# Four gate tiles back in full products, and weight sums left to accumulating DMAs in one projection, in a one-layer hybrid trunk

## The chip, the cores and the metric

The kernel runs on one core of one Trainium2 chip. The metric is the device time of one execution in microseconds (us), less is better. The five engines are named as the profile names them: PE (TensorE, matrix products), DVE (VectorE), ACT (ScalarE), POOL (GpSimd), SP (SyncE, which only issues DMAs here). "SPq" and "POOLq" are DMAs issued by SP and by POOL.

## The reference

One decoder layer in float32 over 512 tokens of width 1024. Cut to what matters here:

```
h = rmsnorm(x, g_mix)
z = h @ w_in                     # 10 groups of 512 columns, then 3 x 1024 columns of gate logits
merged = sum over 3 branches n of sigmoid(gate_n(h) + b_n) * (branch_n(h) @ w_branch[n])
x = x + merged @ w_o
q = rmsnorm(x, g_xa) @ w_xq ; k, v = rmsnorm(mem, g_mem) @ w_xk, w_xv     # 256 memory tokens
p = softmax(q k^T / 16)          # 4 heads of 256
x = x + (p @ v) @ w_xo
x = x + squared_relu(rmsnorm(x, g_mlp) @ w_up) @ w_down
out = rmsnorm(x, g_fin)
```

The three branches are a short convolution ("cv"), a stick-breaking attention ("sb") and a retention ("rt").

## The kernel before, in words

**Precision.** A float32 operand is split into a high and a low part of the type float32r (`hi` is ACT's copy, `lo` is DVE's subtraction of it), and a product is three matmuls: high times high, high times low, low times high. An output tile of 128 rows by 512 columns over 1024 inputs is thus 8 x 3 = 24 matmuls of 512 columns.

**The weights' way.** All weights come in chunks of 512 KB (128 partitions x 1024 elements) through one stream. SP loads a chunk into one of six buffers `w_raw` (line 215). `parts_of` (lines 112 and 113) makes the parts `w_part` from it: ACT copies the high part, DVE subtracts the low one. There are ten buffers `w_part`, so five pairs of parts. The stream is pumped two steps ahead of the item that uses it (`AHEAD`); a list of items (`plan`) gives the order in which the program is written, and a scheduler then orders the instructions of each engine. On the chip every engine runs its own instructions strictly in that order, each waiting at semaphores.

**The seven-product form.** Where a 2 x 2 block product is wanted, it can be done with seven block products in place of eight, for some additions before and after. Two places use it. Class `Seven` (with `seven`, line 322) computes a pair of gate tiles: four 512-element additions on the weights (lines 128 and 131, in `w_raw`), four steps of parts, 84 matmuls of 256 columns and three additions of 256 columns on results. Class `Wide` (with `items_w`, line 380) is used for the projections w_o, w_xo and w_down: for each 1024 x 1024 block, it makes the products P1, P5, P6, P3, P2, P7, P4 in this order. The weights come as four block kinds B11, B12, B22, B21, each in two halves j = 0 and 1; P1 is made of B11, P5 of the B11 buffer after one addition, P6 after another two (one of them on the B12 buffer, for P7), P4 after one more. With two halves that is eight DVE additions of 128 x 1024 (lines 128 and 131) for each block. The left sides (`Pairs.make`, line 358) are combined the same way from results: `pr`, `pr_b` and `pr_v`.

**The gates.** There are 24 gate tiles, 8 for each branch. The first 12 (`G7` = 12) are plain tiles of 24 matmuls each (`gates`, line 899), the last 12 are six pairs in the seven-product form (`gates7`, line 928). Each item also makes its branch product (`w_br`, 12 matmuls for each tile), takes a sigmoid on ACT (lines 906 and 935) and multiplies and adds into the merged tile `mg` on DVE (lines 890 and 891). When two tiles of the last branch are done, `Pairs.make` builds the left sides for w_o from them. The last four tiles are thus directly ahead of w_o's products.

**The memory attention.** The queries' eight tiles, the second half of the values (`xv1`) and the scores of each head are interleaved (lines 1127 to 1142). `xa_scores` ends in DVE's maximum and ACT's exponential, `xa_transpose` in a cast on ACT and a subtraction on DVE, and `xa_out(h)` multiplies with the values, with four ACT copies and `Pairs.make` behind it. `xa_out` of heads 2 and 3 stand at the end, followed by w_xo's products in `proj_norm` (line 1013).

Of the kernel before, what the change touches and what calls it, by code (L numbers as in the profile page):

```python
# [15 lines left out]
P = 128  # L16
# [5 lines left out]
W = 512  # L22
# [11 lines left out]
RAWS, WBUFS, AHEAD = 6, 10, 2  # L34
G7, UP = 12, 8


@with_exitstack
def trunk_kernel(ctx: ExitStack, tc: tile.TileContext, x, mem, par, rot, dqd, kdec, g_mix, g_xa, g_mem, g_mlp,
# [97 lines left out]


    class Seven:

# [34 lines left out]
    class Wide:  # L175

        def __init__(self, t, c):
            self.loads = [(t, c + i) for i in range(8)]  # L180
# [169 lines left out]
    class Pairs:  # L350
# [27 lines left out]
    TO = dict(P1=(0, 0), P2=(0, 0), P3=(0, 1), P4=(2, 0), P5=(2, 1), P6=(0, 1), P7=(2, 1))  # L378

    def items_w(src, c, pairs, after=lambda p: None):  # L380

# [3 lines left out]
        def part(p, js, n):  # L385
            bank = dict(P2="p2", P5="p3", P3="p3").get(p, "p1")

            def fn(ws):
# [14 lines left out]
                def add(i):  # L403
                    t, h = TO[p]
                    dst = S["x"][t + i][:, h * 512:(h + 1) * 512]
                    dve.tensor_tensor(out=dst, in0=acc[bank, i], in1=dst, op=ALU.add)  # L406
# [7 lines left out]
            item(fn, (Wide, src, c, n, n + len(js)))  # L414

# [17 lines left out]

    def items_m(src, c0, a, done, nt=NT, tok_outer=False):

        chunks = [(Plain, src, c0 + i) for i in range(4)]
        if tok_outer:
            pss = {}
            for t in range(nt):
                def mm(*ws, t=t):  # L440
                    pss[t] = mmps()
                    proj_m(pss[t], ws, a(), t, 0, 8)
                item(mm, *chunks)
                item(lambda t=t: done(t, pss[t]))
        else:
            pss = []
            for i in range(4):
                def fn(w, i=i):
                    for t in range(nt):
                        if i == 0:  # L450
                            pss.append(mmps())
                        proj_m(pss[t], [w], a(), t, 2 * i, 8)
                        if i == 3:
                            done(t, pss[t])
                item(fn, chunks[i])

# [442 lines left out]
    def gates(n, name, ds=range(KT)):  # L899
        for d in ds:  # L900
            def fn(wg, wb, d=d):
# [7 lines left out]
                gated(n, d, ps2, gt)  # L909
            item(fn, (Plain, w_in, 40 + n * KT + d), (Plain, w_br, n * 4 + d // 2))  # L910

# [88 lines left out]
    gates7(1, "sb", range((G7 - KT) // 2, KT // 2))  # L1000
    gates7(2, "rt", range(KT // 2))

# [9 lines left out]

    def proj_norm(src, name, g, beside, after):

# [18 lines left out]

        items_w(src, 0, lambda k: S[name, k // 2].w[k % 2], ends)
        after(lambda t: item(lambda: norm_T(t, S["hT"], t)))
# [92 lines left out]
    for i in range(KT + 4):  # L1128
# [56 lines left out]

    proj_norm(w_xo, "xo", g_mlp, lambda p: None, first_up)

# [100 lines left out]
def _lay_out(i):  # L1288
# [16 lines left out]
        "g_mlp": a["norm_mlp_g"][0], "g_fin": a["final_g"],  # L1305
        "w_in": np.concatenate(secs + [_pack_t(w_in[:, 10 * W:10 * W + G7 * P])], axis=0),
        "w_gate": _pack_s(w_in[:, 10 * W + G7 * P:]),
        "w_br": np.concatenate([_pack_b(a["w_branch"][0, n]) for n in range(3)], axis=0),
# [35 lines left out]
```

## Time and profile before

| | us |
|---|---|
| median of 3 runs | 1028.94 (1028.44 to 1029.39) |
| the profiled execution's own time | 1027.97 |
| its span | 1026.3 |
| PE busy | 995.6 (97%) |
| DVE busy | 734.8 (72%) |
| ACT busy | 533.4 (52%) |
| POOL busy | 64.5 (6%) |

The span is that of the profiled execution, from the first to the last instruction shown; 1.67 us of its time lie outside. In the timelines a row is: start, length, engine, line, operation, output from input, shape, count; in brackets stands the idle time of that engine just before the row and what ended it. A row with a count stands for several instructions in a row. In the windows a row is one stretch of the span, with the busy time and the number of instructions of each engine, the granted PE clock (1.00 is full), the busy share of the DMA engines and GB/s. Matmul rows overlap, since they are pipelined: the spacing of starts counts, not the length.

### The profile page before, as it was taken

The page shows a single profiled execution, that of the slowest core. Times are in us where ns is not written, and L with a number is a line of the kernel's source. Part 1 is how long each engine was busy: PE and PEld are TensorE (multiplying, and loading weights), DVE is VectorE, ACT ScalarE, POOL GpSimd, SP SyncE. Part 2 cuts the span into 40 slices and gives each one's busy share as a digit, 9 for nine tenths or more (in the row PEclk, how much of TensorE's full clock was granted, in tenths as well). Part 3 has the DMA queues.
Part 4 walks back from the last instruction along what each step waited for, and adds up shares of the span by engine and source line. Part 5 has one row for each costly group of instructions (what it writes and reads, how often), then busy time and mean ns, then how long its engine had stood idle before and what let it go on. Part 6 is the DMA issues. An engine that isn't in the chain of part 4 may idle for free.

```text
span 1026.3 us, 13274 instructions
## 1 busy us (share of the span) xinstructions
PE 995.6 (97%) x5030; PEld 843.1 (82%) x5030; DVE 734.8 (72%) x1089; ACT 533.4 (52%) x923; POOL 64.5 (6%) x125
## 2 busy tenths in 40 slices
PE   6999999999999999997999998999999999999996
PEld 5888888878888889996798886779888888888885
DVE  5657787778454787799795459785784786696785
ACT  6456666766422345455474446465553553553543
POOL 1000111223110000001100000000000000000001
PEclk9999999999999999999899999999999999999999
DMA  9242223212132113234544210252034125215212
GB/s 365 107 144 82 82 83 118 81 72 80 62 103 82 63 62 108 78 124 173 172 168 165 83 62 21 80 187 82 21 119 169 42 81 169 79 42 185 82 42 82
DMA packets 30448, 107.84 MB, mean 105 GB/s; under 512 B 3760, under 2 KB 3760, under 8 KB 30384
## 3 DMA queue, kind: packets, MB, share of 16 engines
q1 hardware_dynamic: 27648, 99.63, 27.6%
q0 software_dynamic: 1440, 5.24, 1.5%
q10 hardware_dynamic: 1296, 2.13, 0.6%
q8 instruction: 39, 0.64, 0.3%
q14 instruction: 25, 0.20, 0.1%
HBM read 104.89 MB, written 2.10 MB: 104 GB/s over the span
## 4 chain that ended last, share of the span: by engine, by line
PE 93%; DVE 5%; issue 1%; ACT 1%; DMA 0%; POOL 0%; DVEq 0%; POOLq 0%; SPq 0%; ACTq 0%
PE p L400 21%; PE mm L272 20%; PE mm L273 20%; PE mm L274 20%; PE p L330 5%; DVE w_part L113 1%; PE o L712 1%; PE aT L678 1%; PE at L497 1%; PE z L654 0%; DMA w_raw<-in_w_in_dram 0%; PE z L655 0%; DVE w_raw L128 0%; DVE w_raw L131 0%; PE ro L854 0%
## 5 line engine op out<-in xcount | busy, mean ns | idle before, releaser
L113 DVE TENSOR_TENSOR w_part<-w_raw,w_part 128x1024 fp32r<-128x1024 f32 (+1 forms) x228 | 274.7, 1206 | 156.4 <-ACT w_part L112 149.9
L112 ACT CAST w_part<-w_raw 128x1024 fp32r<-128x1024 f32 (+1 forms) x228 | 236.6, 1040 | 269.8 <-PE mm L273 125.8
L273 PE MATMUL mm<-hT_l,w_part 128*128 128x512 f32 (+1 forms) x704 | 268.4, 382 | 1.7 <-DVE hT_l L262 1.7
L272 PE MATMUL mm<-hT_h,w_part 128*128 128x512 f32 (+1 forms) x704 | 268.0, 383 | 1.1 <-DVE r_qk L775 1.1
L274 PE MATMUL mm<-hT_h,w_part 128*128 128x512 f32 (+1 forms) x704 | 268.2, 382 | 0.0
L400 PE MATMUL p<-w_part,pr 128*128 128x512 f32 x864 | 205.5, 394 | 3.8 <-ACT pr L261 2.7
L400 PEld LDWEIGHTS p<-w_part,pr 128*128 128x128 f32 x864 | 162.4, 190 | 40.1 <-ACT pr L261 3.1
L273 PEld LDWEIGHTS mm<-hT_l,w_part 128*128 128x128 f32 x704 | 132.5, 188 | 25.6 <-DVE hT_l L262 1.9
L272 PEld LDWEIGHTS mm<-hT_h,w_part 128*128 128x128 f32 x704 | 132.0, 188 | 25.8 <-DVE r_qk L775 1.7
L274 PEld LDWEIGHTS mm<-hT_h,w_part 128*128 128x128 f32 x704 | 132.5, 188 | 24.6
L406 DVE TENSOR_TENSOR x<-p,x 128x512 f32<-128x512 f32 x84 | 56.8, 684 | 20.4 <-PE p L400 20.2
L400 PE MATMUL p<-w_part,pr_b 128*128 128x512 f32 x144 | 36.9, 411 | 2.4 <-ACT w_part L112 2.0
L128 DVE TENSOR_TENSOR w_raw<-w_raw 128x1024 f32<-128x1024 f32 (+1 forms) x36 | 37.5, 1041 | 0.5
L131 DVE TENSOR_TENSOR w_raw<-w_raw 128x1024 f32<-128x1024 f32 (+1 forms) x36 | 37.4, 1038 | 0.1
L330 PE MATMUL p<-mix_h,w_part 128*128 128x256 f32 x192 | 37.0, 283 | 0.0
L400 PEld LDWEIGHTS p<-w_part,pr_b 128*128 128x128 f32 x144 | 28.5, 199 | 9.4 <-ACT w_part L112 2.4
L666 DVE TENSOR_TENSOR_SCAN sb_suf<-ones,sb_e 128x128 f32<-128x128 f32 (+3 forms) x32 | 27.4, 857 | 9.5 <-POOL sb_e L645 8.2
L272 PE MATMUL mm<-w_part,xg_h 128*128 128x512 f32 x64 | 26.4, 413 | 7.8 <-ACT xg_h L266 7.8
L330 PEld LDWEIGHTS p<-mix_h,w_part 128*128 128x128 f32 x192 | 31.0, 191 | 0.2
L669 ACT ACTIVATE sb_suf<-sb_suf 128x128 f32<-128x128 f32 (+3 forms) x32 | 15.1, 471 | 29.5 <-DVE sb_suf L668 29.4
L330 PE MATMUL p<-hT_h,w_part 128*128 128x256 f32 x144 | 28.6, 283 | 0.4 <-ACT w_part L112 0.4
L330 PE MATMUL p<-mix_l,w_part 128*128 128x256 f32 x96 | 27.1, 283 | 0.0
(237 smaller groups left out, 1457.4 us busy)
## 6 DMA issues: line engine op xcount, KB each, us to landing
w_raw<-in_w_in_dram SPq DMA_DIRECT2D x52, 512.0 KB, 3.3
w_raw<-in_w_up_dram SPq DMA_DIRECT2D x32, 512.0 KB, 4.0
w_raw<-in_w_down_dram SPq DMA_DIRECT2D x32, 512.0 KB, 3.3
w_raw<-in_w_br_dram SPq DMA_DIRECT2D x12, 512.0 KB, 3.3
w_raw<-in_w_gate_dram SPq DMA_DIRECT2D x12, 512.0 KB, 3.3
w_raw<-in_w_o_dram SPq DMA_DIRECT2D x8, 512.0 KB, 3.7
w_raw<-in_w_xk_dram SPq DMA_DIRECT2D x8, 512.0 KB, 3.3
w_raw<-in_w_xv_dram SPq DMA_DIRECT2D x8, 512.0 KB, 4.2
```

The lines of the kernel that those rows point to most:

```text
L112: act.copy(out=wh, in_=src)
L113: dve.tensor_tensor(out=wl, in0=src, in1=wh.bitcast(F32), op=ALU.subtract)
L128: dve.tensor_tensor(out=out, in0=a, in1=b, op=ALU.subtract)
L131: dve.tensor_tensor(out=out, in0=a, in1=b, op=ALU.add)
L272: te.matmul(ps, lh, rh, start=first, stop=False)
L273: te.matmul(ps, lh, rl, start=False, stop=False)
L274: te.matmul(ps, ll, rh, start=False, stop=last)
L330: te.matmul(ps[:, :256], x[:, k, :], y, start=first and k == 0 and i == 0, stop=k == 3 and i == 2, skip_group_check=True)
L400: te.matmul(acc[bank, i], x, y, start=p in ("P1", "P5", "P2") and j + k + m == 0, stop=j == 1 and k == 1 and m == 2, skip_group_check=True)
L406: dve.tensor_tensor(out=dst, in0=acc[bank, i], in1=dst, op=ALU.add)
L666: dve.tensor_tensor_scan(out=suf[:, :s][:, ::-1], data0=ones[:, :s], data1=e1[:, :s][:, ::-1], initial=0.0, op0=ALU.mult, op1=ALU.add)
L669: act.activation(out=suf[:, :s], in_=suf[:, :s], func=AF.Exp)
```

## The change

There are four edits.

1. `G8` = 20. The tiles 12 to 19 stay in the seven-product form, the last four (branch "rt", d = 4 to 7) are computed as plain tiles again. Their weights move from the tensor `w_gate` to `w_in`, in the same number of bytes.
2. In the seven-product form of the three projections the weights are only added, never subtracted. The signs move to the left sides (`neg`, one `scalar_tensor_tensor` in place of one `tensor_tensor`) and to the additions of the results (`TO` has an operation now).
3. A new class `Summed`, used for w_xo alone. A DVE addition between two weight blocks is replaced by a DMA that POOL issues: it reads the second block from DRAM again and adds it to the buffer `w_raw`, in which the first block lies. There are eight of these, of 512 KB each. Such a DMA may start when the parts of the buffer's former content have been made, and the next parts may be made when it has landed.
4. `xa_out(2)` and `xa_out(3)` move from ahead of w_xo's products to between its first and its second item (P1 with j = 0, and P5 with j = 0).

```diff
-G7, UP = 12, 8
+G7, G8, UP = 12, 20, 8
...
             if p == "P5":
-                minus(b11, b12, b11)
+                plus(b11, b11, b12)
             elif p == "P6":
-                plus(b11, b22, b11)
+                plus(b11, b11, b22)
                 plus(b12, b12, b22)
             elif p == "P4":
-                minus(b11, b21, b11)
+                plus(b11, b11, b21)
             return parts_of(dict(P3=b22, P2=b21, P7=b12).get(p, b11))
+
+    class Summed(Wide):
+        def __init__(self, t, c):
+            super().__init__(t, c)
+            self.need = [n + (n in (1, 3)) for n in self.need]
+
+        def step(self, raw, p, j):
+            b11, b12, b22, b21 = (raw[i] if i < len(raw) else None for i in (2 * j, 2 * j + 1, 4 + j, 6 + j))
+
+            def acc(dst, i):
+                pool.dma_start(out=dst, in_=self.t[self.c + i], accum_op=ALU.add)
+
+            parts = parts_of(dict(P3=b22, P2=b21, P7=b12).get(p, b11))
+            if p == "P1":
+                acc(b11, 2 * j + 1)
+                acc(b12, 4 + j)
+            elif p in ("P5", "P6"):
+                acc(b11, 4 + j if p == "P5" else 6 + j)
+            return parts
...
+            def neg(out, a, b):
+                dve.scalar_tensor_tensor(out=out, in0=a, scalar=-1.0, in1=b, op0=ALU.mult, op1=ALU.subtract)
+
             v = scr("pr_v", (P, 2, 256))
-            minus(v, u[:, 0:1, :].broadcast_to([P, 2, 256]), s)
+            minus(v, s, u[:, 0:1, :].broadcast_to([P, 2, 256]))
             put(("A11", "A22"), s)
-            minus(u[:, 0, :], s[:, 0, :], v[:, 1, :])
+            neg(u[:, 0, :], s[:, 0, :], v[:, 1, :])
             put(("S3", "S1"), v)
...
-            minus(u[:, 1, :], u[:, 1, :], u[:, 0, :])
+            neg(u[:, 1, :], u[:, 1, :], u[:, 0, :])
...
-    gates7(2, "rt", range(KT // 2))
+    gates7(2, "rt", range((G8 - 2 * KT) // 2))
+    gates(2, "rt", range(G8 - 2 * KT, KT))
...
-    item(lambda: xa_out(2))
-    item(lambda: xa_out(3))
+
+    def last_heads(its):
+        plan.append(its.pop(0))
+        item(lambda: xa_out(2))
+        item(lambda: xa_out(3))
+        plan.append(its.pop(0))
...
-    proj_norm(w_xo, "xo", g_mlp, lambda p: None, first_up)
+    proj_norm(w_xo, "xo", g_mlp, lambda p: None, first_up, last_heads, Summed)
```

**What moves.** The first place is DVE at the end of the gates. Before, with the last pair's weights in the buffers 3828 and 3830:

```order
L131 TENSOR_TENSOR w_raw_3828<-w_raw_3830,w_raw_3828 128x512
L262 TENSOR_TENSOR pr_3990<-mg_2676,pr_3990 128x512
L128 TENSOR_TENSOR w_raw_3828<-w_raw_3830,w_raw_3828 128x512
L346 TENSOR_TENSOR sv_u_4026<-p3_4024,sv_u_4026 128x256
L113 TENSOR_TENSOR w_part_4172<-w_raw_3828,w_part_4171 128x1024
L344 TENSOR_TENSOR sv_s_4025<-p1_4022,sv_s_4025 128x256
L113 TENSOR_TENSOR w_part_4176<-w_raw_3830,w_part_4175 128x1024
L113 TENSOR_TENSOR w_part_4184<-w_raw_3836,w_part_4183 128x1024
L890 TENSOR_TENSOR gt_4135<-mm_4138,gt_4135 128x512
L113 TENSOR_TENSOR w_part_4190<-w_raw_4003,w_part_4189 128x1024
L891 TENSOR_TENSOR mg_2809<-mg_2809,gt_4135 128x512
```

After, with the buffers 3836 and 3842, of which 3842 is the first that belongs to w_o:

```order
L910 TENSOR_TENSOR gt_4031<-mm_4033,gt_4031 128x512
L288 TENSOR_TENSOR pr_3985<-pr_v_3979,pr_3985 128x512
L393 SCALAR_TENSOR_TENSOR mg_2676<-mg_2676 128x256
L911 TENSOR_TENSOR mg_2809<-mg_2809,gt_4031 128x512
L113 TENSOR_TENSOR w_part_4121<-w_raw_3842,w_part_4120 128x1024
L910 TENSOR_TENSOR gt_4079<-mm_4081,gt_4079 128x512
L288 TENSOR_TENSOR pr_3991<-mg_2676,pr_3991 128x512
L131 TENSOR_TENSOR w_raw_3842<-w_raw_3842,w_raw_3994 128x1024
L911 TENSOR_TENSOR mg_2809<-mg_2809,gt_4079 128x512
L131 TENSOR_TENSOR w_raw_3994<-w_raw_3994,w_raw_4112 128x1024
```

The four 512-element additions on the last pair's weights and the result additions of lines 342 to 346 are gone; between the subtractions of line 113 there now stand mostly the gates' multiplications (line 910, formerly 890) and the left sides (lines 288 and 393), and the first two additions for w_o (line 131) stand three and five rows behind the low part of w_o's first block (4121).

The second place is POOL from the queries' norm to the norm behind w_xo. Before:

```order
L460 TENSOR_TENSOR rstd_4746<-ms_4744,half_78 128x1
L460 TENSOR_TENSOR rstd_4752<-ms_4750,half_78 128x1
L94 DMA g_bc_6039<-in_g_mlp_dram 128x1024
L460 TENSOR_TENSOR rstd_6096<-ms_6094,half_78 128x1
L460 TENSOR_TENSOR rstd_6102<-ms_6100,half_78 128x1
```

After:

```order
L480 TENSOR_TENSOR rstd_4630<-ms_4628,half_78 128x1
L480 TENSOR_TENSOR rstd_4636<-ms_4634,half_78 128x1
L213 DMA w_raw_5394<-in_w_xo_dram 128x1024
L213 DMA w_raw_5557<-in_w_xo_dram 128x1024
L213 DMA w_raw_5329<-in_w_xo_dram 128x1024 x2
L213 DMA w_raw_5492<-in_w_xo_dram 128x1024 x2
L213 DMA w_raw_5329<-in_w_xo_dram 128x1024
L213 DMA w_raw_5492<-in_w_xo_dram 128x1024
L94 DMA g_bc_5925<-in_g_mlp_dram 128x1024
L480 TENSOR_TENSOR rstd_5982<-ms_5980,half_78 128x1
```

The eight DMAs of line 213 are the accumulations into the B11 buffers (5329 and 5492, three each) and the B12 buffers (5394 and 5557). They stand ahead of the load of the next norm's gain `g_bc` on the same engine.

The third place is ACT around the last casts of the values, `xv_h`, in the memory attention. Before, with 5445 and 5608 as the two B11 buffers of w_xo:

```order
L112 CAST w_part_5890<-w_raw_5608 128x1024
L1092 ACTIVATE x_p_5709,x_sm_5710<-xsc_5693,x_mx_5706 128x256 x2
L261 CAST xpT_5669<-xpp_5716 128x2x256
L261 CAST xv_h_4356<-mm_5679 128x512
L112 CAST w_part_5909<-w_raw_5608 128x1024
L261 CAST xv_h_4357<-mm_5686 128x512
L112 CAST w_part_5929<-w_raw_5445 128x1024
L261 CAST xpT_5769<-xpp_5764 128x2x256
L1092 ACTIVATE x_p_5757,x_sm_5758<-xsc_5741,x_mx_5754 128x256 x2
L1123 COPY xo_s_5820<-mm_5822 128x256
L1124 COPY xo_u_5821<-mm_5822 128x256
L1123 COPY xo_u_5821<-mm_5831 128x256
L1124 COPY xo_s_5820<-mm_5831 128x256
```

After, with 5329 and 5492 as the two B11 buffers:

```order
L112 CAST w_part_5684<-w_raw_5329 128x1024
L112 CAST w_part_5705<-w_raw_5492 128x1024
L1116 ACTIVATE x_p_5593,x_sm_5594<-xsc_5577,x_mx_5590 128x256 x2
L287 CAST xpT_5553<-xpp_5600 128x2x256
L1116 ACTIVATE x_p_5641,x_sm_5642<-xsc_5625,x_mx_5638 128x256 x2
L112 CAST w_part_5796<-w_raw_5492 128x1024
L287 CAST xv_h_4240<-mm_5563 128x512
L112 CAST w_part_5815<-w_raw_5329 128x1024
L287 CAST xv_h_4241<-mm_5570 128x512
L287 CAST xpT_5653<-xpp_5648 128x2x256
L287 CAST xpT_5653<-xpp_5677 128x2x256
L112 CAST w_part_5834<-w_raw_5492 128x1024
L1147 COPY xo_s_5726<-mm_5728 128x256
L1148 COPY xo_u_5727<-mm_5728 128x256
```

The casts of P5, P1 (j = 1), P5 (j = 1) and P6 (line 112) stand at much the same places among the casts of `xpT`, `xv_h` and the copies of the heads; all but P1's now read buffers that an accumulating DMA writes.

More of the change, by code (lines that the diff above doesn't have):

```diff
@@ L179, in __init__ @@
         def __init__(self, t, c):
+            self.t, self.c = t, c
             self.loads = [(t, c + i) for i in range(8)]
@@ L372, in make, with items_w @@
             split(hi, lo, u[:, 1, :])
-            minus(u[:, 1, :], u[:, 1, :], u[:, 0, :])
+            neg(u[:, 1, :], u[:, 1, :], u[:, 0, :])
             put(("S2", "S4"), u)
     LEFT = dict(P1="A11", P2="A12", P3="S4", P4="A22", P5="S1", P6="S2", P7="S3")
-    TO = dict(P1=(0, 0), P2=(0, 0), P3=(0, 1), P4=(2, 0), P5=(2, 1), P6=(0, 1), P7=(2, 1))
-    def items_w(src, c, pairs, after=lambda p: None):
+    TO = dict(P1=(0, 0, plus), P2=(0, 0, plus), P3=(0, 1, minus), P4=(2, 0, plus), P5=(2, 1, minus), P6=(0, 1, minus),
+              P7=(2, 1, minus))
+    def items_w(src, c, pairs, after=lambda p: None, kind=Wide):
         acc = {}
@@ L403, in add @@
                 def add(i):
-                    t, h = TO[p]
+                    t, h, op = TO[p]
                     dst = S["x"][t + i][:, h * 512:(h + 1) * 512]
-                    dve.tensor_tensor(out=dst, in0=acc[bank, i], in1=dst, op=ALU.add)
+                    op(dst, dst, acc[bank, i])
                 rows = p in ("P7", "P4")
@@ L432, in proj_m, with items_m, fn @@
                 mm3(ps, ah[:, sl], al[:, sl], wh[:, j, :], wl[:, j, :], k == 0, k == nk - 1)
[L434 to L455, printed above, removed]
+    def items_m(src, c0, a, done, nt=NT):
+        pss = []
+        for i in range(4):
+            def fn(w, i=i):
+                for t in range(nt):
+                    if i == 0:
+                        pss.append(mmps())
+                    proj_m(pss[t], [w], a(), t, 2 * i, 8)
+                    if i == 3:
+                        done(t, pss[t])
+            item(fn, (Plain, src, c0 + i))
     def rstd_of(ms, n):
@@ L1011, in reload_x, with proj_norm @@
         S["x"] = load_x()
-    def proj_norm(src, name, g, beside, after):
+    def proj_norm(src, name, g, beside, after, first=lambda its: None, kind=Wide):
         def ends(p):
@@ L1032, in ends @@
             beside(p)
-        items_w(src, 0, lambda k: S[name, k // 2].w[k % 2], ends)
+        its = capture(lambda: items_w(src, 0, lambda k: S[name, k // 2].w[k % 2], ends, kind))
+        first(its)
+        plan.extend(its)
         after(lambda t: item(lambda: norm_T(t, S["hT"], t)))
```

9 lines of the change are left out of this document (5 added, 4 removed).

## The prediction

> **What bounds the kernel now.** I read the page's shares first, then the chain of waits, then PE's timeline and the windows around the two places that the change touches.
>
> ```profile
> PE 995.6 (97%) x5030; PEld 843.1 (82%) x5030; DVE 734.8 (72%) x1089; ACT 533.4 (52%) x923; POOL 64.5 (6%) x125
> ...
> PE 93%; DVE 5%; issue 1%; ACT 1%; DMA 0%; POOL 0%; DVEq 0%; POOLq 0%; SPq 0%; ACTq 0%
> ```
>
> PE sets the time nearly everywhere, and only 5% of the chain goes over DVE. So time is to be had in two ways: fewer PE cycles, or a stretch in which PE waits for DVE. The cost of PE work is read off long runs in the chain of waits (start, length, what):
>
> ```profile
> 432.10 8.63 PE p L330 x72
> ...
> 745.32 32.64 PE p L400 x144
> ```
>
> A 512-column matmul costs 32.64/144 = 0.2267 us, a 256-column one 8.63/72 = 0.1199 us. Where PE waits, its timeline shows. The end of the gates and the first products of w_o:
>
> ```profile
> 475.61 2.79 PE L400 MATMUL p<-w_part,pr 128*128 128x512 f32 x11 [0.34 <-ACT gt L935]
> 481.09 2.90 PE L400 MATMUL p<-w_part,pr 128*128 128x512 f32 x10 [2.69 <-ACT pr L261]
> 484.19 0.73 PE L400 MATMUL p<-w_part,pr 128*128 128x512 f32 x2 [0.21 <-DVE pr L262]
> 486.94 1.22 PE L400 MATMUL p<-w_part,pr_b 128*128 128x512 f32 x2 [2.01 <-ACT w_part L112]
> 488.54 4.62 PE L400 MATMUL p<-w_part,pr_b 128*128 128x512 f32 x10 [0.38 <-DVE w_part L113]
> 492.97 4.28 PE L400 MATMUL p<-w_part,pr 128*128 128x512 f32 x18
> ```
>
> From 475.61 to the start of P6 at 492.97, 17.36 us, PE issues 11+10+2+2+10 = 35 matmuls, 7.9 us at 0.2267. So 9.4 us are lost. What DVE and the clock do meanwhile stands in the windows:
>
> ```profile
> 476.00:480.00 4.00, 2.40 (x11) 1.64 (x9) 4.00 (x6) 1.78 (x3) 0.00 (x0) 1.00 0.00 0
> 480.00:484.00 4.00, 2.84 (x10) 1.72 (x10) 4.00 (x7) 2.71 (x4) 0.00 (x0) 1.00 0.09 18
> 484.00:488.00 4.00, 1.79 (x4) 0.80 (x4) 4.00 (x6) 1.67 (x2) 0.00 (x0) 0.77 0.62 222
> 488.00:492.00 4.00, 3.62 (x9) 2.82 (x9) 4.00 (x6) 0.00 (x0) 0.00 (x0) 0.50 0.45 153
> 492.00:496.00 4.00, 4.00 (x17) 3.21 (x17) 1.31 (x3) 1.05 (x1) 0.00 (x0) 0.87 0.01 4
> ```
>
> DVE is busy for 4.00 of 4 us while PE is not: it is the bound here. And the granted clock falls to 0.50. (0.23+0.50+0.13) x 4 us x 2 = 6.9 us ran at half clock; the ten matmuls at 488.54 took 4.43 us to the next row's start in place of 2.27. About 2.4 us of the 9.4 are the clock's, 7 are waits.
>
> The second place is w_xo's start, with the last values and heads:
>
> ```profile
> 634.70 0.73 PE L274 MATMUL mm<-xpT,xv_l 128*128 128x512 f32 x2 [0.73 <-DVE xv_l L262]
> 639.18 0.66 PE L1104 MATMUL xpp<-ident,x_p 128*128 128x128 f32 x2 [3.75 <-DVE x_p L1096]
> 639.50 5.88 PE L400 MATMUL p<-w_part,pr 128*128 128x512 f32 x17
> ...
> 655.43 2.94 PE L400 MATMUL p<-w_part,pr 128*128 128x512 f32 x11 [0.42 <-DVE pr L262]
> ```
>
> ```profile
> 635.00:640.00 5.00, 1.25 (x5) 0.82 (x4) 5.00 (x10) 2.85 (x9) 0.00 (x0) 0.64 0.00 0
> 640.00:645.00 5.00, 5.00 (x17) 3.89 (x16) 1.69 (x4) 1.59 (x2) 0.00 (x0) 0.68 0.00 0
> ```
>
> Again DVE is full (5.00 of 5) while PE has 1.25, and the clock is halved behind it: (0.36+0.32) x 5 x 2 = 6.8 us. The three waits make 4.9 us, the clock some 1.9 (17 matmuls in about 5.7 us, not 3.85), the tails of the matmuls ahead of the gaps the rest: about 7.3 us lost before P6 of w_xo starts at about 655.9.
>
> **The change, part by part.**
>
> *Four plain gate tiles.* On PE a pair costs 48 x 0.2267 = 10.9 us in full products, 84 x 0.1199 = 10.1 in seven. Two pairs: **+1.6 us**, with nothing to hide it. What DVE is spared stands in the groups by shape from 425 to 500 us:
>
> ```profile
> L113 DVE TENSOR_TENSOR w_part<-w_raw,w_part 128x1024 fp32r<-128x1024 f32 x19 | 23.1, 1218 | 5.0 <-ACT w_part L112 5.0
> ...
> L128 DVE TENSOR_TENSOR w_raw<-w_raw 128x512 f32<-128x512 f32 x4 | 2.7, 685 | 0.0
> ...
> L113 DVE TENSOR_TENSOR w_part<-w_raw,w_part 128x512 fp32r<-128x512 f32 x2 | 1.4, 692 | 0.8 <-ACT w_part L112 0.7
> L346 DVE TENSOR_TENSOR sv_u<-p,sv_u 128x256 f32<-128x256 f32 x3 | 1.3, 419 | 0.6 <-PE p L330 0.6
> ```
>
> For a seven-product pair: four additions of 0.685, one low part of 0.69 and three of 1.22, three result additions of 0.42, together 8.3 us. A plain pair has two low parts, 2.4. Two pairs free 11.8 us of DVE by lengths, some 11 by the closer spacing of starts. The 7 us of waits depend on DVE, so more is freed than lost; but a second limit is behind it. P2's first weight block, made ahead of P6 in both orders, is loaded last:
>
> ```profile
> 482.62 3.34 SPq L215 DMA_DIRECT2D w_raw<-in_w_o_dram  x2
> ```
> ```profile
> 485.84 1.04 ACT L112 CAST w_part<-w_raw 128x1024 fp32r<-128x1024 f32 x1 [0.72 <-DMA w_raw<-in_w_o_dram]
> ```
>
> The load goes out when a buffer is free (482.62), the cast follows at 485.84, the subtraction after that. I laid the new order out by hand with these lengths. By spacings alone PE has P5 (j = 1) behind it at 481.2 (the extra 1.6 is in that). The load is then already there, but the cast needs the two part buffers that P5 holds: high part at 483.1, low part at 485.2 (one other DVE operation of 1.13 between). PE waits 1.9 and 1.6 us, and P6 starts at about 487.5: **-5.5 us** against 492.97, the 1.6 included. If the half clock comes again in these 6.9 us, with PE busy through it, it takes 3.4 back: **-2.1**. Before, it followed on waits of 2.69 and 2.01 us within 8 us, and in w_xo on 0.73 and 3.75. Waits of 1.9 and 1.6 us that close together look like the first of these, so I take -2.1 and keep -5.5 for the range.
>
> The sign changes cost nothing: one 256-column DVE operation is swapped for another, as many as before.
>
> *Eight accumulating DMAs.* They spare DVE eight additions of 1.21 us in w_xo; six of these stand ahead of 640 us, in the stretch where PE waits:
>
> ```profile
> L131 DVE TENSOR_TENSOR w_raw<-w_raw 128x1024 f32<-128x1024 f32 x4 | 4.9, 1214 | 0.0
> ...
> L128 DVE TENSOR_TENSOR w_raw<-w_raw 128x1024 f32<-128x1024 f32 x2 | 2.4, 1214 | 0.0
> ```
>
> That is 7.3 us off a DVE that is full, about the whole loss. The price is a wait: parts, accumulate, parts, in series. No row shows an accumulating DMA. Its time d from issue to landing is bounded by the plain ones of the same size:
>
> ```profile
> w_raw<-in_w_xo_dram SPq DMA_DIRECT2D x8, 512.0 KB, 3.2
> ...
> x<-in_x_dram POOLq DMA_DIRECT2D x4, 512.0 KB, 5.4
> ...
> g_bc<-in_g_xa_dram POOLq DMA_DIRECT2D x1, 512.0 KB, 7.1
> g_bc<-in_g_mlp_dram POOLq DMA_DIRECT2D x1, 512.0 KB, 4.0
> ```
> ```profile
> 468.00:472.00 4.00, 4.00 (x30) 3.78 (x30) 4.00 (x7) 2.21 (x5) 1.60 (x3) 1.00 0.98 366
> ```
>
> Below: 3.2 us, the plain load by SP. Above: 7.1 plus a whole second transfer behind it, 3.2: 10.3. I take 4.0 (a lone load by POOL) plus 512 KB more at the 366 GB/s of the busiest window, 1.4, since the target is read as well: **d = 5.4**, which is also the row of four loads in a run.
>
> The Trainium skill ("DMA: Bandwidth & Descriptors", section "Anatomy of one DMA — SWDGE (gpsimd) path") fits a DMA of this path with 2.0 us and its bytes over 436 GB/s. As an estimate that gives 3.2 us for 512 KB and 4.4 with the target counted, and my sum below would be some 1.7 us better; the row of 4.0 for a plain load lies above the 3.2.
>
> The chain starts at P1's first parts:
>
> ```profile
> 614.03 1.05 ACT L112 CAST w_part<-w_raw 128x1024 fp32r<-128x1024 f32 x1 [3.97 <-PE mm L273]
> ```
> ```profile
> 615.12 1.23 DVE L113 TENSOR_TENSOR w_part<-w_raw,w_part 128x1024 fp32r<-128x1024 f32 x1 [3.60 <-ACT w_part L112]
> ```
>
> The addition for P5 goes out at 616.4 and lands at 621.8; cast and subtraction to 624.0; P1 (j = 1) to 625.8; its addition lands at 631.2, P5 (j = 1) has parts at 633.4; the next addition lands at 638.8 and P6 (j = 1) is cast until 639.8. These casts stand in ACT's order ahead of `xv_h`, `xpT` and the copies of head 2, which wait with them, and DVE and POOL are in order too. In this stretch PE has the two heads' 24 matmuls and the 24 of P1 and P5 (j = 0) to do. By spacings it then waits 1.6 us at P1 (j = 1) and 1 to 1.5 at P5 (j = 1), and P6 starts at about 650.6: **-5.3** against 655.9. By the same layout d = 4.5 gives 648.9, 6 gives 652, 8 gives 656 to 658, 10 gives 664. *The moved heads* are in these figures; alone they only give PE P1's 12 matmuls (2.7 us) ahead of the wait. P4's two additions, late and long landed, free 2.3 us of DVE where PE does not wait: nothing. The gain's load stands behind the eight DMAs on POOL, is issued at about 640 to 645 by this layout and takes 4.0 us; it is first read in the norm behind P3, which comes after P6's 48 matmuls (10.9 us): nothing.
>
> Sum against the profiled execution: 1027.97 - 2.1 - 5.3 = 1020.6. That execution lies 0.97 below the median 1028.94, so about **1021.5** as a median.
>
> **The rivals.**
>
> *The clock stays up behind the gates.* Then the first term is -5.5 and the second stays: 1028.94 - 5.5 - 5.3 = 1018.1. For it: the longest wait falls from 2.69 to 1.9 us. Against it: in the windows above the clock fell though PE had been busy 2.84 and 1.79 of 4 us. The Trainium skill ("TensorE: Matmul & The Clock Gate", section "Part 1: The HAM clock gate (the "warmup" mystery)") ties the half clock to windows of 3.4 us of PE's activity; by its warning against idle gaps longer than that, no wait in the new layout would bring it. The trace of before does not agree, with half clock behind gaps of 2.01 and 2.69 us.
>
> *The accumulations take 7 to 8 us.* Then the series of three eats what DVE gains, and w_xo's P6 is where it was: 1028.94 - 2.1 - 0 to 1 = 1026.4.
>
> *They take longer and the change loses.* The same series at d = 10 puts P6 at 664, +8: 1028.94 - 2.1 + 8 = 1034.8. The place is ACT's cast of P5 (j = 1), behind which the value casts queue; from d = 8.6 on the whole is slower (7.5 if the half clock recurs). For it: 7.1 us for a plain load in one row, and that the two DMAs for P7 go out on the same queue just before. Against it: the DMA engines are idle at 635 to 645 (0 GB/s).
>
> *The gates' end is not relieved.* The part buffers and the last load set P6 of w_o wherever DVE is, the extra 1.6 us is paid, and of w_xo's gain some 1 to 2 us remain: about 1028.
>
> **How the numbers follow.** The forecast has 0.40, the clock that stays up 0.22, the accumulations of 7 to 8 us 0.15, the slower case 0.14, no relief 0.09. About 0.2%, 2 us, is what a measurement of this kernel can tell from no change. Faster: 0.40 + 0.22 + half of 0.15 + 0.02 of the last = 0.72. Slower: 0.14 + 0.01. Same: 0.13. The forecast's own range is 1019.5 to 1024 (d from 4.5 to 6.5, half clock partly). The range runs from 1016.5 (both gains in full, d at 4.5) to 1029, which leaves out the slower case.
>
> **What the changed profile would show.** The accumulate's row from issue to landing, 4.5 to 6.5 us, decides the second term. In w_o, P6 starts near 487.5 at full clock or 491 at half; the wait for P2's cast remains, at about 2 us, and DVE has idle time between 476 and 492. In w_xo, DVE is no longer full at 630 to 640, ACT's casts of P5 and P6 are ended by a DMA, and P6 starts about 5 us earlier relative to the queries' projection. A half clock at 481 to 495 tells the forecast from its first rival. The forecast is wrong if ACT's casts wait more than 4 us for a DMA while PE waits for `xv_h`, or if P6 of w_o starts no earlier than before.

## The result

| | before | after |
|---|---|---|
| median, us | 1028.69 (4 runs, 1027.80 to 1029.39) | 1018.91 (4 runs, 1018.13 to 1020.44) |
| profiled execution, us | 1027.97 | 1020.44 |
| its span, us | 1026.3 | 1018.7 |

The ratio is 0.9913, with a 95% interval of 0.9901 to 0.9925: faster by about 9 us (the two medians are 9.8 us apart). The forecast was 1021.5 with a range of 1016.5 to 1029; the first rival, with a clock that stays up, was at 1018.1. The measured time lies between the two, 0.6 us below the forecast's own narrower range of 1019.5 to 1024.

PE's timeline after the change, at the end of the gates and the first products of w_o (P1 and P5 are the 48, then half of P2, then P6):

```profile
469.97 11.04 PE L430 MATMUL p<-w_part,pr 128*128 128x512 f32 x48
482.38 0.73 PE L430 MATMUL p<-w_part,pr_b 128*128 128x512 f32 x2 [1.36 <-ACT w_part L112]
484.48 3.87 PE L430 MATMUL p<-w_part,pr_b 128*128 128x512 f32 x10 [1.37 <-DVE w_part L113]
488.14 4.16 PE L430 MATMUL p<-w_part,pr 128*128 128x512 f32 x16
```

P1 and P5 run without a wait now, and two waits for P2's parts are left. P6 starts at 488.14 in place of 492.97, **4.8 us** earlier. Of this, 0.4 us lies ahead of the place: the last branch's first product with `rt_out` starts at 410.48 in place of 410.90. The windows there:

```profile
476.00:480.00 4.00, 4.00 (x20) 3.30 (x19) 2.93 (x6) 1.72 (x3) 0.00 (x0) 1.00 0.25 76
480.00:484.00 4.00, 1.75 (x7) 0.81 (x5) 3.68 (x4) 1.85 (x3) 0.00 (x0) 1.00 0.49 160
484.00:488.00 4.00, 3.52 (x10) 2.79 (x11) 3.98 (x6) 0.04 (x1) 0.00 (x0) 0.68 0.46 160
488.00:492.00 4.00, 4.00 (x17) 3.24 (x17) 1.80 (x2) 1.00 (x1) 0.00 (x0) 0.89 0.17 52
```

PE is busy for all of 476 to 480, where it had 2.40 us before. The half clock (a granted clock of 0.50) is back, but shorter: (0.32 + 0.11) x 4 x 2 = 3.4 us of it, where 6.9 had been. The ten matmuls at 484.48 take 3.66 us instead of 2.27, so it costs 1.4 us there.

The DMA view and POOL's timeline show the new transfers (the first row: median us from issue to landing at its end; the others: the first, third and eighth of the eight):

```profile
w_raw<-in_w_xo_dram POOLq DMA_DIRECT2D x8, 512.0 KB, 5.2
```
```profile
575.47 0.93 POOL L213 DMA_DIRECT2D w_raw<-in_w_xo_dram  x1 [53.55 <-DVE x_sm L1118]
...
612.66 0.87 POOL L213 DMA_DIRECT2D w_raw<-in_w_xo_dram  x1 [22.10 <-DVE w_part L113]
...
638.61 0.88 POOL L213 DMA_DIRECT2D w_raw<-in_w_xo_dram  x1 [5.08 <-DVE w_part L113]
```

ACT's casts of weights at the start of w_xo (P1; P5; P1 and P5 with j = 1 third and fourth; P6 with j = 1), and PE's waits up to P6, with which the row of 48 begins:

```profile
610.05 1.05 ACT L112 CAST w_part<-w_raw 128x1024 fp32r<-128x1024 f32 x1 [3.98 <-PE mm L299]
617.88 1.05 ACT L112 CAST w_part<-w_raw 128x1024 fp32r<-128x1024 f32 x1 [1.21 <-PE xsc L300]
619.73 1.05 ACT L112 CAST w_part<-w_raw 128x1024 fp32r<-128x1024 f32 x1 [0.80 <-PE mm L299]
628.32 1.05 ACT L112 CAST w_part<-w_raw 128x1024 fp32r<-128x1024 f32 x1 [3.04 <-DMA w_raw<-in_w_xo_dram]
...
636.00 1.05 ACT L112 CAST w_part<-w_raw 128x1024 fp32r<-128x1024 f32 x1 [3.74 <-DMA w_raw<-in_w_xo_dram]
```
```profile
642.79 2.83 PE L430 MATMUL p<-w_part,pr 128*128 128x512 f32 x10 [0.85 <-ACT pr L287]
646.04 0.73 PE L430 MATMUL p<-w_part,pr 128*128 128x512 f32 x2 [0.42 <-DVE pr L288]
647.24 11.22 PE L430 MATMUL p<-w_part,pr 128*128 128x512 f32 x48 [0.47 <-DVE x L131]
```

From P1's cast to P6 it is 647.24 - 610.05 = 37.2 us; before it was 655.9 - 614.03 = 41.9. That is **4.7 us**. Two casts do wait for an accumulating DMA, for 3.0 and 3.7 us, but PE waits for neither: the largest wait left is 0.85, where 3.75 was. DVE is no longer full there, and the half clock that followed the old wait (6.8 us) does not come, so part of the 4.7 us, some 1.9 by the prediction's reading of before, is the clock's:

```profile
630.00:635.00 5.00, 5.00 (x24) 3.94 (x23) 4.16 (x6) 2.26 (x4) 1.73 (x2) 1.00 0.55 95
635.00:640.00 5.00, 5.00 (x24) 4.12 (x23) 2.91 (x5) 3.82 (x9) 1.39 (x2) 1.00 0.63 116
```

The two gains make 9.5 us and the span is 7.6 shorter. Of the rest, 0.85 went between P6 of w_o and w_xo's first cast (121.9 us in place of 121.1; the half clock's end in P6 and a wait of 0.38), and 1.1 behind P6 of w_xo, in the norm. There PE waits equally long in both kernels, and only the second execution was given a half clock behind it:

```profile
688.55 0.38 PE L273 MATMUL mm<-hT_l,w_part 128*128 128x256 f32 x1 [1.74 <-DVE hT_l L262]
```
```profile
679.81 0.44 PE L299 MATMUL mm<-hT_l,w_part 128*128 128x256 f32 x1 [1.75 <-DVE hT_l L288]
```
```profile
680.00:690.00 10.00, 10.00 (x73) 10.00 (x73) 3.86 (x10) 1.61 (x5) 0.54 (x1) 0.83 0.21 72
```

The first row is the kernel before, the second and the window are after (0.17 x 10 x 2 = 3.4 us at half clock). The profiled execution is the slowest of the four: their granted clocks were 0.995, 0.997, 0.998 and 0.998, their times 1020.44, 1019.49, 1018.34 and 1018.13.

### The profile page after: what moved, and what is told of

Same layout as the page of the kernel before. It is cut to its first block, busy times and chain, and to the rows that moved or that the text cites. A ratio compares the mean times of both kernels' runs of the same rounds, so it can differ in the third digit from the quotient of the medians.

```text
span 1018.7 us, 13121 instructions
## 1 busy us (share of the span) xinstructions
PE 994.7 (98%) x4958; PEld 840.6 (83%) x4958; DVE 717.3 (70%) x1063; ACT 527.3 (52%) x909; POOL 73.7 (7%) x133
## 5 line engine op out<-in xcount | busy, mean ns | idle before, releaser
L299 PE MATMUL mm<-hT_l,w_part 128*128 128x512 f32 (+1 forms) x736 | 281.8, 383 | 1.7 <-DVE hT_l L288 1.7
L300 PE MATMUL mm<-hT_h,w_part 128*128 128x512 f32 (+1 forms) x736 | 281.6, 383 | 0.0
L298 PE MATMUL mm<-hT_h,w_part 128*128 128x512 f32 (+1 forms) x736 | 280.5, 384 | 1.1 <-DVE r_qk L795 1.1
L299 PEld LDWEIGHTS mm<-hT_l,w_part 128*128 128x128 f32 x736 | 139.4, 189 | 26.9 <-DVE hT_l L288 1.9
L300 PEld LDWEIGHTS mm<-hT_h,w_part 128*128 128x128 f32 x736 | 139.4, 189 | 25.6
L298 PEld LDWEIGHTS mm<-hT_h,w_part 128*128 128x128 f32 x736 | 138.3, 189 | 27.0 <-DVE r_qk L795 1.8
L131 DVE TENSOR_TENSOR w_raw<-w_raw 128x1024 f32<-128x1024 f32 (+1 forms) x48 | 54.3, 1131 | 0.7 <-DMA w_raw<-in_w_down_dram 0.3
L128 DVE TENSOR_TENSOR x<-x,p 128x512 f32<-128x512 f32 x48 | 32.6, 683 | 9.5 <-PE p L430 9.5
L298 PE MATMUL mm<-w_part,xg_h 128*128 128x512 f32 x64 | 26.4, 413 | 7.6 <-ACT xg_h L292 7.6
L131 DVE TENSOR_TENSOR x<-x,p 128x512 f32<-128x512 f32 x36 | 24.1, 682 | 11.5 <-PE p L430 11.4
L299 PE MATMUL mm<-w_part,xg_h 128*128 128x512 f32 x64 | 25.8, 404 | 0.0
L356 PE MATMUL p<-mix_h,w_part 128*128 128x256 f32 x128 | 25.0, 283 | 0.0
L300 PE MATMUL mm<-w_part,xg_l 128*128 128x512 f32 x64 | 24.3, 389 | 0.0
L486 ACT ACTIVATE xn<-x 128x512 f32<-128x512 f32 x24 | 15.1, 629 | 15.8 <-DVE x L131 8.0
```

The lines of the kernel that those rows point to most:

```text
L128: dve.tensor_tensor(out=out, in0=a, in1=b, op=ALU.subtract)
L131: dve.tensor_tensor(out=out, in0=a, in1=b, op=ALU.add)
L298: te.matmul(ps, lh, rh, start=first, stop=False)
L299: te.matmul(ps, lh, rl, start=False, stop=False)
L300: te.matmul(ps, ll, rh, start=False, stop=last)
L356: te.matmul(ps[:, :256], x[:, k, :], y, start=first and k == 0 and i == 0, stop=k == 3 and i == 2, skip_group_check=True)
```

## The experiments

The kernel before had medians of 1028.42, 1027.78, 1027.51 and 1028.13 us in the four groups of runs (e1 to e4; e5 to e7; e8 to e10; e11). The changed kernel was not timed again in them under its own name (but see e3).

### The gates alone

```diff
-    proj_norm(w_xo, "xo", g_mlp, lambda p: None, first_up, last_heads, Summed)
+    item(lambda: xa_out(2))
+    item(lambda: xa_out(3))
+    proj_norm(w_xo, "xo", g_mlp, lambda p: None, first_up)
```

> The four plain gate tiles and the sums-only signs alone; the attention's output projection adds on DVE and the last heads stand ahead of it, as before. Theory (two separate gains, each where DVE was full while PE waited): P6 of w_o starts about 4.8 us earlier than before, w_xo is as before: about 1024 us (1022 to 1025.5) against 1028.7 before and 1018.9 with all parts. Rival (the end of the gates gives nothing, all comes from w_xo): 1028 us or more, as PE has 1.6 us more to do.

Measured: 1023.92 us, ratio 0.9955 (0.9943 to 0.9967), that is -4.5 us by the medians, as the theory had it. P6 of w_o started at 488.10. The run shows that the gates' edit gives this time. That it gives it through DVE's time, and not through something else in which the two forms differ, rests on the windows and on e6; it was not tried by itself.

### w_xo alone

```diff
-G7, G8, UP = 12, 20, 8
+G7, G8, UP = 12, 24, 8
```

> All twelve late gate tiles stay in the seven-product form; the accumulating DMAs and the moved heads alone. Theory: P6 of w_xo starts 4.5 to 5.5 us earlier relative to P1's first cast, the end of the gates is as before (waits of 2 to 3 us, half clock): about 1024 us (1022.5 to 1025). Rival (accumulations as slow as 7 us or more, the gain comes from the gates): 1028 us. Second rival (the two gains are one, a half clock that is shed): 1020 us.

Measured: 1024.61 us, ratio 0.9955 (0.9942 to 0.9968), -4.6 by the ratio and -3.8 by the medians. From P1's first cast to P6 of w_xo it is 652.68 - 615.25 = 37.4 us, 4.4 less than before. The two ratios multiply to 0.9910, the whole change has 0.9913: two separate gains of about the same size, and no third.

### The heads back, the sums by DMA

```diff
-    proj_norm(w_xo, "xo", g_mlp, lambda p: None, first_up, last_heads, Summed)
+    item(lambda: xa_out(2))
+    item(lambda: xa_out(3))
+    proj_norm(w_xo, "xo", g_mlp, lambda p: None, first_up, kind=Summed)
```

> All of the change but the moved heads: the last two heads stand ahead of w_xo's first product again, the sums are by DMA. Theory (the heads are cover for the wait on the accumulations of P5): PE does the same work earlier and then waits at P5 or P1 (j = 1) for parts; P6 of w_xo starts 1 to 3 us later, 1020 to 1022 us. Rival (the heads' place carries the gain in w_xo): 1023.5 us or more. Third (place is of no matter, as the chain of casts sets P6): 1018.9 us within 0.7.

Measured: 1018.70 us (6 runs, 1017.51 to 1023.32), ratio 0.9912 (0.9896 to 0.9928). The third: it makes no difference. The reason is plainer than the one I gave: with buffer numbers and line numbers left out, the instructions of all five engines stand in the same order as in the changed kernel. The scheduler had put the last heads there anyway. So this is the changed kernel once more, and its profile shows what the clock adds. In its timeline P2's waits are nearly the same as in the first fence of the result:

```profile
482.59 0.73 PE L430 MATMUL p<-w_part,pr_b 128*128 128x512 f32 x2 [1.41 <-ACT w_part L112]
484.65 2.56 PE L430 MATMUL p<-w_part,pr_b 128*128 128x512 f32 x10 [1.33 <-DVE w_part L113]
487.04 11.04 PE L430 MATMUL p<-w_part,pr 128*128 128x512 f32 x48
```

No stretch between 440 and 700 us is below full clock in this execution (1017.51 us, clock 0.998); the ten matmuls take 2.39 us and P6 starts 1.1 us earlier still.

### The heads moved, the sums on DVE

```diff
-    proj_norm(w_xo, "xo", g_mlp, lambda p: None, first_up, last_heads, Summed)
+    proj_norm(w_xo, "xo", g_mlp, lambda p: None, first_up, last_heads, Wide)
```

> All of the change but the DMAs: w_xo's eight additions are on DVE again, the heads stay between P1 and P5. Theory (DVE's seven us of additions are the gain): DVE is full again at the start of w_xo and PE waits there 3 us or more; 1022.5 to 1024.5 us. Rival (the heads' place carries the gain): 1019 to 1020.5 us.

Measured: 1024.20 us, ratio 0.9960 (0.9948 to 0.9972), within 0.3 us of the gates alone, whose order of instructions it shares (numbers left out). Without the DMAs the old wait is back in PE's timeline:

```profile
635.28 0.41 PE L1128 MATMUL xpp<-ident,x_p 128*128 128x128 f32 x2 [3.75 <-DVE x_p L1120]
```

So all of w_xo's gain comes from the DMAs. (The heads' place may matter in a program in which the scheduler would not choose it; that was not tried.)

### The signs alone

```diff
-G7, G8, UP = 12, 20, 8
+G7, G8, UP = 12, 24, 8
...
-    proj_norm(w_xo, "xo", g_mlp, lambda p: None, first_up, last_heads, Summed)
+    item(lambda: xa_out(2))
+    item(lambda: xa_out(3))
+    proj_norm(w_xo, "xo", g_mlp, lambda p: None, first_up)
```

> The sums-only signs alone: weights are added, never subtracted, the left sides and the result additions carry the signs; gates, additions by DVE and the heads' place as before. Theory (one DVE operation for another of the same shape): no change, 1027 to 1029.5 us. Rival (the swapped operation is slower): more than 1030 us.

Measured: 1027.76 us, ratio 1.0000 (0.9991 to 1.0009). No change, as laid out.

### The price of the series doubled

```diff
             def acc(dst, i):
-                pool.dma_start(out=dst, in_=self.t[self.c + i], accum_op=ALU.add)
+                for _ in range(2):
+                    pool.dma_start(out=dst, in_=self.t[self.c + i], accum_op=ALU.add)
```

> Each accumulating DMA of w_xo is issued twice in a row into the same buffer (the block is added twice, so the output is another one). This doubles the price in the series parts, accumulate, parts. Theory (three accumulations in series, some 2 us of slack in all): the cast of P5 (j = 1) comes some 8 to 10 us later and the value casts behind it in ACT's order with it; P6 of w_xo 8 to 13 us later, 1027 to 1032 us, no longer faster than before (1028.4). Rival (the series is covered by other work): 1019 to 1021 us.

Measured: 1029.70 us (10 runs), ratio 1.0030 (1.0016 to 1.0043): the change becomes a loss, 10.8 us above the changed kernel's median. ACT's cast of P5 (j = 1), the first row, comes 29.6 us behind P1's cast (609.04) in place of 18.3, and P6 45.9 behind it in place of 37.2. PE waits for a left side and for P1's addition to x, which ACT and DVE reach late behind such casts:

```profile
638.66 1.99 ACT L112 CAST w_part<-w_raw 128x1024 fp32r<-128x1024 f32 x2 [5.20 <-DMA w_raw<-in_w_xo_dram]
```
```profile
642.45 7.39 PE L431 MATMUL p<-w_part,pr 128*128 128x512 f32 x24 [2.31 <-ACT pr L288]
654.93 13.81 PE L431 MATMUL p<-w_part,pr 128*128 128x512 f32 x48 [5.09 <-DVE x L131]
```

### A little more for each link

```diff
                 pool.dma_start(out=dst, in_=self.t[self.c + i], accum_op=ALU.add)
+                pool.dma_start(out=dst[:, :128], in_=self.t[self.c + i][:, :128], accum_op=ALU.add)
```

> Behind each accumulating DMA a second one of 64 KB into the first 128 columns of the same buffer (added twice there, so the output is another one): a small addition to the price, about 2.5 to 3.5 us for each link of the series. Theory: 1022 to 1026 us, between the change and no gain in w_xo (1024.2), about what the layout gave for accumulations of 8 us. Rival (covered): 1019 to 1020 us.

Measured: 1027.86 us (10 runs), ratio 0.9998 (0.9989 to 1.0006), worse than I expected: 64 KB more for each link cost 9 us, almost as much as 512 KB. POOL's timeline tells why (the rows from the third pair on; line 213 is the whole accumulation, 214 the small one):

```profile
612.11 0.86 POOL L213 DMA_DIRECT2D w_raw<-in_w_xo_dram  x1 [16.68 <-DVE w_part L113]
617.53 0.86 POOL L214 DMA_DIRECT2D w_raw<-in_w_xo_dram  x1 [4.56 <-DMA w_raw<-in_w_xo_dram]
622.90 0.87 POOL L213 DMA_DIRECT2D w_raw<-in_w_xo_dram  x1 [4.50 <-DVE x_sm L1119]
624.76 0.87 POOL L213 DMA_DIRECT2D w_raw<-in_w_xo_dram  x1 [0.99 <-DVE w_part L113]
628.31 0.87 POOL L214 DMA_DIRECT2D w_raw<-in_w_xo_dram  x1 [2.68 <-DMA w_raw<-in_w_xo_dram]
631.17 0.87 POOL L214 DMA_DIRECT2D w_raw<-in_w_xo_dram  x1 [1.99 <-DMA w_raw<-in_w_xo_dram]
```

The first link takes 5.4 us to the small one's issue and 2.7 (its median) to landing: 8.1, as meant. But the next two accumulations are in flight together, and POOL is in order: the small one of the second buffer (631.17) goes out only behind the wait for the first buffer's (628.31). That is read from the order on POOL; it was not tried with the two on separate queues. The second of these links is 631.17 + 2.7 - 624.76 = 9.1 us or more. Waits of PE for 3.14 and 2.54 us follow. So little of the price is covered by other work, and each wait on POOL's queue belongs to it. Part of the 9 us may be the clock's: from 630 to 700 us this execution has 10.3 us of half clock (the run before it 10.2), the changed kernel 3.4, and each microsecond of it costs a busy PE half of one.

### One plain pair instead of two

```diff
-G7, G8, UP = 12, 20, 8
+G7, G8, UP = 12, 22, 8
```

> Only the last pair of gate tiles is plain, ten of the twelve late tiles stay in the seven-product form: 0.8 us less of PE, 5.5 us instead of 11 of DVE freed. Theory (DVE's excess at the end of the gates is about 7 us, so one pair frees most of it): P6 of w_o within 1.5 us of the change's, 1018 to 1020.5 us. Rival (both pairs are needed): 1021.5 us or more, halfway to 1024.6.

Measured: 1022.04 us, ratio 0.9941 (0.9928 to 0.9954). The theory missed on the time and the rival is right: both pairs are needed. Windows of this kernel, and PE's row of the ten matmuls ahead of P6:

```profile
476.00:480.00 4.00, 2.80 (x13) 1.99 (x11) 4.00 (x8) 2.54 (x3) 0.00 (x0) 1.00 0.40 162
480.00:484.00 4.00, 2.65 (x6) 1.65 (x7) 4.00 (x8) 2.49 (x4) 0.00 (x0) 0.65 0.36 131
484.00:488.00 4.00, 3.72 (x9) 2.15 (x7) 4.00 (x6) 1.67 (x2) 0.00 (x0) 0.50 0.05 9
```
```profile
488.67 2.60 PE L430 MATMUL p<-w_part,pr_b 128*128 128x512 f32 x10 [0.40 <-DVE w_part L113]
```

DVE is still full to 488 us, and PE still waits for it: these ten matmuls start at 488.67, where the change starts them at 484.48. The half clock is back for (0.35 + 0.50) x 4 x 2 = 6.8 us, and P6 starts at 491.10. That is 3.0 us later than in the change, of which 1.3 were there already at the first product with `rt_out` (411.78 against 410.48). So 5.5 us off DVE did not empty it, though PE's waits had come to no more than 7. That buffers covered the rest of DVE's excess is the likely reason; it was not shown.

### The accumulating DMAs in w_o too

```diff
-    proj_norm(w_o, "mp", g_xa, mem_beside, kv_proj)
+    proj_norm(w_o, "mp", g_xa, mem_beside, kv_proj, kind=Summed)
```

> The accumulating DMAs in w_o as well as in w_xo. DVE is spared another 9 us, but there the blocks come late: P1's first part is cast shortly before PE wants it, and three accumulations of some 5 us and three pairs of parts then stand in series ahead of P6's second half. Theory: PE waits 5 us or more for these, 1022 to 1030 us. Rival (DVE's additions are still what P6 of w_o waits for): 1016 to 1018 us.

Measured: 1025.57 us, ratio 0.9971 (0.9960 to 0.9982), 6 to 7 us worse than the change. The wait of PE is there, but behind something I had not named:

```profile
490.11 4.93 PE L430 MATMUL p<-w_part,pr 128*128 128x512 f32 x12 [7.05 <-DVE x L131]
```
```profile
481.91 0.87 POOL L213 DMA_DIRECT2D w_raw<-in_w_o_dram  x1 [4.47 <-DVE w_part L113]
482.45 2.46 POOL L100 DMA_DIRECT2D x<-in_x_dram  x4
```

PE waits for P1's addition into x, and x itself is reloaded by POOL, behind the eight accumulations: at 482, where the change does it between 441 and 464. The next run takes that away.

### w_o too, with x reloaded earlier

```diff
     gates(2, "rt", range(G8 - 2 * KT, KT))
+    plan.insert(len(plan) - 2, ((), lambda: S.update(x=load_x())))
...
-    item(reload_x)
...
-    proj_norm(w_o, "mp", g_xa, mem_beside, kv_proj)
+    proj_norm(w_o, "mp", g_xa, mem_beside, kv_proj, kind=Summed)
```

> As the run before with accumulating DMAs in w_o too, but the reload of x is written two items earlier, so that on POOL it stands between the accumulations instead of behind all of them. There P1's addition to x had kept PE waiting for 7.05 us. Theory (that wait was POOL's order, not the sums): it is gone, P6 of w_o starts near 483 to 485 us instead of 488.1 in the change, as the products before it were done at 483.1; 1014 to 1017.5 us. Rival (the series of accumulations sets P6 of w_o whatever comes behind it): 1019 us or more.

Measured: 1025.49 us, ratio 0.9977 (0.9965 to 0.9989): the same time with other waits. The first waits are gone and P6 begins at 481.75, as hoped; then P2's parts are late.

```profile
481.75 2.97 PE L430 MATMUL p<-w_part,pr 128*128 128x512 f32 x12 [0.62 <-DVE x L131]
...
497.13 0.73 PE L430 MATMUL p<-w_part,pr_b 128*128 128x512 f32 x2 [2.63 <-ACT w_part L112]
```
```profile
484.14 2.94 ACT L112 CAST w_part<-w_raw 128x1024 fp32r<-128x1024 f32 x3 [4.83 <-DMA w_raw<-in_w_o_dram]
...
496.04 1.04 ACT L112 CAST w_part<-w_raw 128x1024 fp32r<-128x1024 f32 x1 [4.08 <-DMA w_raw<-in_w_o_dram]
```

ACT's casts wait 4 to 5 us for DMAs, and one of these is P2's block. The first of the two waits is for an accumulation, issued at 478.63 and landed at 484.06; P3's casts stand behind it in the row of three. The second is for P2's plain load, which SP issues at 488.21, when DVE has made P3's low part and a buffer is free:

```profile
488.21 2.06 SPq L241 DMA_DIRECT2D w_raw<-in_w_o_dram  x2
```
```profile
490.00:495.00 5.00, 4.50 (x20) 3.38 (x18) 3.39 (x7) 1.95 (x8) 1.67 (x3) 1.00 1.03 279
```

That load takes 7.8 us to land, 3.2 in the change: the DMA engines are full, with POOL's loads of `g_bc` and `m_sb` and two accumulations in flight (10.6 and 12.8 us from issue to landing). So POOL's order was one cause. The next is the series, which delays P2's load through ACT's order, and the full DMA engines, which stretch it.

### w_o too, all twelve late tiles in seven products

```diff
-G7, G8, UP = 12, 20, 8
+G7, G8, UP = 12, 24, 8
...
+    plan.insert(len(plan) - 4, ((), lambda: S.update(x=load_x())))
...
-    item(reload_x)
...
-    proj_norm(w_o, "mp", g_xa, mem_beside, kv_proj)
+    proj_norm(w_o, "mp", g_xa, mem_beside, kv_proj, kind=Summed)
```

> Accumulating DMAs in both projections, x reloaded ahead of them, and all twelve late gate tiles in the seven-product form: DVE is spared w_o's additions instead of the gates', PE has 1.6 us less to do than in the change. Theory (at the end of the gates P1's parts of w_o come late from a full DVE, and the series of three accumulations starts from there): P6 of w_o at about 490 us, 1020 to 1024 us. Rival (any 9 us off DVE are worth the same there): 1013 to 1016 us.

Measured: 1030.79 us, ratio 1.0028 (1.0017 to 1.0038): slower than before, by more than I expected. PE waits 2.69 us at 472.27 and 2.08 at 481.51, both for casts, and P6 starts at about 492. Time off DVE is not worth the same in each form: in w_o it is bought with a series of accumulations, which took up to 8.8 us each there. How the loss comes about in this run was not followed further.

### P2 last in w_o

```diff
-                        acc[bank, i] = (mmps if p == "P2" else atps)(bank)
+                        acc[bank, i] = (mmps if p == "P2" and src is not w_o else atps)(bank)
```

> The change with one more edit: in w_o P2's two result banks are taken from the four banks that P1 and P3 use, not from those of the plain products. P2 can then only start when P3's banks are free, and PE takes P6 straight behind P5, with P2's 24 matmuls behind P7 and P4; the sum is the same. Theory (what is left of the loss at the end of the gates is the wait for P2's parts, 1.36 + 1.37 us, and the half clock behind it): P6 starts at 481 to 483 us in place of 488.1, 1015 to 1017.5 us. Rival (P2's parts then hold two of five pairs of buffers through P7 and P4, the wait moves there): 1018.5 us or more.

Measured: 1024.97 us, ratio 0.9970 (0.9960 to 0.9980), 6 us worse than the change. The rival is right that it loses, though not where it said:

```profile
486.17 16.69 PE L430 MATMUL p<-w_part,pr 128*128 128x512 f32 x62 [4.06 <-DVE x L131]
...
534.32 1.09 PE L517 MATMUL at<-ident,xn 128*128 128x128 f32 x8 [2.06 <-DVE hT_l L288]
```

P6 cannot follow P5 at once, since its bank holds P1's result until DVE has added it to x: PE waits 4.06 us there, more than for P2's parts (1.36 + 1.37). And the norm, which needs P2's sum, then ends late (2.06). Between 480 and 495 us it has 6.8 us of half clock, the change 3.4. The order that the scheduler had chosen was the better one.

## Why the prediction was right, and where it was not

**What bounds the kernel** was read rightly: two stretches in which DVE was full and PE waited. Each part relieves one of them, by 4.6 us in a run of its own (by the ratios; 4.5 and 3.8 by the medians), and together they give the whole.

**The gates' end.** P6 at 487.5 was laid out at full clock, 488.14 came with some half clock and 487.04 without (in e3, the same program). The two waits for P2's parts were put at 1.9 and 1.6 us and are 1.36 and 1.37. The term that was mis-sized is the half clock: I took back 3.4 us for a full return of 6.9 us of it; it took 1.4 in the profiled execution and nothing in others. The term is -4.5 in place of -2.1. The second term was 0.7 us too large, so the two errors cancel in part; that the forecast came as near as 2.6 us owes something to this. The +1.6 us of PE is in it and was not measured by itself.

**The accumulations.** d was taken as 5.4 us from the lone POOL load and a second transfer; 5.2 was measured. Counted from P1's first cast, the layout had the three accumulations of the series land at 7.8, 17.2 and 24.8 us and P6 start at 36.6; the trace has 7.8, 18.2, 25.9 and 37.2. P6 was put at -5.3; it is -4.7 in the trace and -4.6 by e2. The cast of P5 (j = 1) waits for its DMA, as laid out, and the value casts behind it do not hold PE up. What failed here is where PE waits: the 1.6 us at P1 (j = 1) and 1 to 1.5 at P5 (j = 1) do not come, and instead there are 0.85, 0.42 and 0.47 ahead of P6, for left sides and for x. The two DMAs for P7, counted for a rival as going out just before, are issued at 575.47 and 589.69, far ahead of the series.

**The moved heads** were a step that failed. I gave them a place in the layout and said that alone they give PE cover. They change nothing here: the order of the instructions is the same without the edit. The orders shown ahead of the prediction are those of the whole change, and can't tell which edit moved what.

**The rivals.** The clock that stays up (1018.1) is close to the truth for some executions. Accumulations of 7 us or more were refuted (5.0 to 5.9 for the eight), and the slower case lives at the price I gave it or below: it was to decide from d = 8.6 on, and links of about 8 to 9 us already cost all of w_xo's gain and the gates' beside it (1027.86). I had left POOL's order out of that price. "The gates' end is not relieved" was refuted by e1.

**The clock rule.** The Trainium skill ("TensorE: Matmul & The Clock Gate", section "Part 1: The HAM clock gate (the "warmup" mystery)") says that the activity window runs freely and does not start with the kernel, so that the point of a transition varies. The traces fit that: one order of instructions with waits of 1.36 + 1.37 us was given 3.4 us of half clock in one execution, and with 1.41 + 1.33 none in another. Its warning against gaps above 3.4 us is too mild for this case, as half clock follows on gaps half as long (1.36 and 1.37 us, and a single one of 1.75).

## What to carry to other kernels

Where a second engine is full while the first waits, look for the work of that engine that can be had in another form right there, and pay with what is cheap there: here 1.6 us of a PE that waited, and DMA engines that had nothing to do. A DMA in a series parts, transfer, parts costs its latency each time. It paid where the chain starts early and other work lies beside it (w_xo), and in none of the three forms tried where the blocks come late (w_o); the order of everything else on the issuing queue belongs to its price. How much has to be taken off the full engine can't be read from the waits alone: half the relief at the gates (e6, ratio 0.9941) left DVE full and brought about a third of what the whole of it did (0.9955 without, 0.9913 with). That share is rough, since each ratio is known to 0.0013; by the medians it is 2.6 of 5.7 us.

## What the hardware showed that was not expected

An accumulating DMA of 512 KB took 5.2 us from issue to landing, against 3.3 for the plain loads of the same tensor by SP. POOL needed 0.87 to 0.97 us to issue one, and 0.54 to 0.58 for most plain loads. Behind plain loads on POOL's queue, with the DMA engines full, two accumulations took 10.8 and 12.8 us to land (e8). The DMA engines were busier for the same traffic (after the change, in w_xo; at the end of the row the busy share and GB/s):

```profile
620.00:625.00 5.00, 5.00 (x31) 4.42 (x30) 3.46 (x9) 2.91 (x9) 1.84 (x2) 1.00 0.61 105
```

That is a share of 0.61 at 105 GB/s, where plain loads of the kernel before had 0.33 at 116 GB/s (440 to 450 us). And the half clock came behind waits as short as 1.36 and 1.37 us in a row, or did not, in the same program. Where it came, it came in pieces of about 3.4 us: between 470 and 720 us the executions have none (e3), 3.4 (e8), 6.8 (after, e1, e4, e7), 10.2 to 10.3 (e2, e6, both runs of e5, e11), 13.6 (before, e10) and 17.0 us (e9) of it.
